# Input projection: other order of its pieces beside the hyena and the heads, and modulation's weights 1 MB at a time

## The chip, the cores and the metric

The kernel runs on one core of a Trainium2 chip. Its engines, TensorE (PE), VectorE (DVE), ScalarE (ACT), GpSimd (POOL) and SyncE (SP, which issues DMAs), each run their own queue in order and wait for one another by semaphores. The metric is the device time of one execution in microseconds (us).

## What is computed

One layer of a hybrid token mixer and an MLP, for 1024 latent and 256 context tokens of width 1024, in float32. One input projection feeds three groups: a Hyena long convolution, gated linear attention (GLA, 4 heads) and gated DeltaNet (GDN, 4 heads). GDN's q, k and v go through a convolution of 7 taps. Shifts, scales and gates (modulation) come from two vectors through `w_mod`.

```python
sh1, sc1, g1, sh2, sc2, g2 = jnp.split((silu_c @ w_mod[l] + b_mod[l])[:, None, :], N_MOD, axis=-1)
h = modulate(x, norm1_g[l], sh1, sc1)
...
zl_hy, zl_gla, zl_gdn = split_last(h @ w_in, IN_SIZES)
zc_hy, zc_gla, zc_gdn = split_last(hc @ w_in, IN_SIZES)
hy_lat = hyena_mix(zl_hy, rows, GRID_W, hy_conv_w, hy_conv_b, hyena_filters(h.shape[1], *hy_filter), hy_d)
gla_lat, gla_ctx = gla_branch(zl_gla, zc_gla, with_ctx_out, gla_w_a2, gla_b_a, gla_norm_g)
gdn_lat, gdn_ctx = gdn_branch(zl_gdn, zc_gdn, rows, with_ctx_out, gdn_conv_w, gdn_a_log, gdn_dt_bias, gdn_norm_g)
y_lat = jnp.concatenate([hy_lat, gla_lat, gdn_lat], axis=-1) @ w_out
...
x = x + g1 * y
x = x + g2 * sq_relu_mlp(modulate(x, norm2_g[l], sh2, sc2), w_mlp1[l], w_mlp2[l])
# inside gdn_prep: qkv = silu(short_conv(qkv, conv_w)); q, k l2-normed; inside the scan: solve (I - A) X = rhs, chunk by chunk
```

## The kernel before, in words

**Pieces.** The input projection is cut into 28 pieces of 128 output columns: hy0 to hy5 (hyena), gk, gv, gq, gg (GLA's k, v, q, gate), dk, dv, dq, dg (GDN's). `proj` makes a piece: `load_w` (L302) loads 512 KB of weights into `ws`, splits them into a rounded `wh` (ACT) and a rest `wl` (POOL), and PE sums three products (`mm3`) over 8 tiles of k into psum tiles `psb`, of which there are three. The latent tokens are two chunks of 512 columns, 24 matmuls each; pieces k and v have the context's 256 columns as a third chunk of 24. Pieces without convolution (`gla_piece`, `gate_piece`) are copied from psb by ACT. Pieces dq, dk and dv (`gdn_conv`, `taps`) start with an Identity by ACT, then DVE adds six taps for each chunk (`acc<-psb,vecs,acc`), ACT does a Silu, and `to_tokens` transposes the result on PE into the single psum tile `psd`, from where ACT copies it. A psb tile is free only when its last tap is done. `acc` has two buffers.

**Stages.** After the norm and the six hyena pieces come, in `run`:
1. the hyena (`long_conv` twice: DFT matmuls into `pss`, their operands made by ACT as `wrh` and DVE or POOL as `wrl`, sums `y` on DVE), with the first string of `SEQ` beside it, and after each piece two steps of modulation (`MODN`). A step of `mod_group` takes one tile of k: it loads weights into `mw` (SP's queue) and multiplies them on PE, four matmuls into one psum tile `psd` (of pool psm); after eight steps the sum is transposed into `modT`.
2. the four heads of GDN (`gdn_prep`), with the second string of `SEQ` (a digit is a head). `gdn_rows` first loads GDN's gates (`NT<-dz_gk`, SP's queue) and makes decays. A head loads k and q tokens, ACT makes 20 exps of 128x128 for either direction (`NT<-NT,cols`, `dm<-dm,cols`), and five rounds follow: k and q are transposed into `psp`, copied as `KQ` by ACT, multiplied into `psp`, and DVE makes `NT<-psp,dm` and `dm<-psp,dm` of it.
3. the inverse of all heads' triangular blocks (copies `i<-NT` on DVE and ACT, then many small matmuls into `psi`), with the third string as filler: a digit is one of the four decays of GLA (`gla_decays`, `acc<-acc` and a scan at L756), dg and gg are gates.
4. GLA, GDN's loops, the output projection and the MLP.

**What sets the order.** The code gives each instruction a priority by where it is written; taps and what follows them are moved ahead by `URGENT`. A scheduler then lays out each engine's queue by priorities and by when operands and buffers are expected to be ready. So a new order in `SEQ` moves instructions on all engines. Pools are closed at the end of a stage; tiles of a pool take turns (`mw`: two buffers of 128x1024).

Of the kernel before, what the change touches and what calls it, by code (L numbers as in the profile page):

```python
# [7 lines left out]
F32 = mybir.dt.float32  # L8
# [179 lines left out]
ENGC = {'eqf': 'vp', 'eqr': 'vp', 'qh0': 'vp', 'qh1': 'vp', 'ekf': 'vp', 'ekr': 'vp', 'kk': 'vp', 'qd0': 'avp', 'qd1': 'avp', 'A': 'va', 'te': 'vp', 'ke': 'vp', 'kt': 'va', 'A2': 'pva', 'q2': 'vp', 'og': 'va', 'ov': 'vp', 'mid': 'pva', 'pk': 'vp', 'pq': 'vp', 'tri': 'vp', 'KQ': 'va', 'C': 'avp', 'off': 'vp', 'Y': 'pva', 'T32': 'pva', 'Ya': 'vp', 'V': 'va', 'V64': 'va', 'pu': 'va', 'NT': 'avp', 'Yh': 'avp', 'V128': 'va', 'sp1': 'vp', 'sp0': 'vp', 'spc': 'vp', 'sps': 'vp', 'wl': 'vp', 'yg': 'vp', 'Sl': 'vp', 'ft': 'vp', 'oq': 'vp', 'qs': 'av', 'S2': 'avp', 'pl': 'vp', 'xr': 'vp', 'kd': 'vp', 'u': 'av'}  # L188
SEQ = ('gk1 gv0 dk0 dq0 gk0 dk1 dv2 gv1 dq1 dk2 gq0 dq2', '0 1 2 dv0 gq1 3 dv1 gv2', 'dg1 0 gg1 gg0 dg0 3 1 gg2 2 dg2')
MODN = 2  # L190
# [21 lines left out]
class Build:  # L212
# [99 lines left out]
    def run(self):  # L312
        tc, nc = self.tc, self.nc
        self._cst, self.y, self.nT, self.nS, self.rooms = {}, [], 0, 0, {i: i - 9 for i in range(4)}
        with ExitStack() as es:
# [38 lines left out]
            close(p0)  # L354
            h, mw = tp("hy", 1, True), tp("mw", 2, True)
            self.H = h[1]
# [82 lines left out]
    def mod_group(self, g, psum, pname, wpool, wnames):  # L439

        nc = self.nc
        ps = psum.tile([128, 512], F32, name=pname)
        for kt in range(8):
            for hf in range(2):
                w = wpool.tile([128, 1024], F32, name=wnames[hf])
                nc.sync.dma_start(w, self.I["wmod"][g, kt, hf])
                for q2 in range(2):
                    q = 2 * hf + q2
                    self.mm(ps[32 * q:32 * q + 32, :], self.cs32[:, kt, :], w[:, 512 * q2:512 * q2 + 512], kt == 0, kt == 7)
            yield  # L450
        ms = wpool.tile([128, 1024], F32, name=wnames[0])[:, :512]
        nc.scalar.copy(ms, ps)
# [10 lines left out]
    def mod_rest(self, psum, pool):  # L463

        for g in (1, 2):
            yield from self.mod_group(g, psum, "psd", pool, ("mw", "mw"))
        self.stt(self.A2, self.modT[:, 32:40, 0], 1.0, self.vec("n2"), ADD, MUL)
        for g in (20, 44):
            self.ts(self.modT[:, g:g + 4, 0], self.modT[:, g:g + 4, 0], -1.0, MUL)
        self.show("modT", self.modT)  # L470
        yield
# [1336 lines left out]
```

## Time and profile before

| | us |
|---|---|
| three runs | 1642.22, 1645.13, 1649.15 |
| median | 1645.13 |
| the profiled execution | 1637.75 |
| its span in the trace | 1636.0 |
| PE, DVE, ACT, POOL busy in the span | 1507.8, 1211.8, 803.2, 642.4 |

The profile is of one execution, so durations are set against its own time. "busy" of PE is the time in which a matmul is in the array; PEclk is the granted clock as a share of full speed (0.953 over the execution). A wait is put down to the instruction whose semaphore came last. In the trace, the hyena and the pieces beside it run from some 195 us to 366 us, the rest of the pieces and the heads to 577, the inverse to 690, and all that follows to the end.

### The profile page before, as it was taken

Reading aid. Unit: us, or ns where it says so; the run is one execution under the profiler, and the core shown is the slowest. Engines: PE = TensorE matmul, PEld = TensorE weight load, DVE = VectorE, ACT = ScalarE, POOL = GpSimd, SP = SyncE. Lnnn points to the kernel's source line nnn. Section 1 sums busy time; section 2 is a strip of 40 time slices with the busy share of each in tenths; the row PEclk is TensorE's granted clock in tenths of the full one; section 3 lists DMA queues with packets and bytes.
Section 4 is the critical chain, followed back from the end, with each engine's and each line's share of the span. In section 5 each row is a group of like instructions: output and inputs, shape, how many; then the busy total and the mean of one; then the engine's idle time right before and its main releaser. Section 6 shows DMA issues by size and latency. Waiting matters only on the chain. (4 is left out here: it accounts for less than half of the span.)

```text
span 1636.0 us, 26277 instructions
## 1 busy us (share of the span) xinstructions
PE 1507.8 (92%) x10160; PEld 1216.2 (74%) x10160; DVE 1211.8 (74%) x1827; ACT 803.2 (49%) x1462; POOL 642.4 (39%) x478
## 2 busy tenths in 40 slices
PE   7799999989999898768879799999999999999996
PEld 2378877767688676657779587788888888888886
DVE  5963589897575487676678878987679758974995
ACT  5432222315655644454556356554565456446554
POOL 0311141331434330131243254655556555655554
PEclk9999999999999997778889899999999999999998
DMA  8432777756566531267657934364455535453532
GB/s 296 135 110 91 259 256 263 238 180 210 165 205 197 165 134 46 75 192 209 182 148 226 309 103 104 103 155 129 104 132 124 149 87 153 103 136 96 135 72 103
DMA packets 116852, 256.81 MB, mean 157 GB/s; under 512 B 29431, under 2 KB 74919, under 8 KB 103800
## 3 DMA queue, kind: packets, MB, share of 16 engines
q1 hardware_dynamic: 88360, 175.42, 32.4%
q0 software_dynamic: 9808, 59.77, 16.4%
q10 hardware_dynamic: 18560, 19.94, 4.0%
q8 instruction: 80, 1.31, 0.3%
q14 instruction: 44, 0.36, 0.1%
HBM read 196.57 MB, written 41.75 MB: 146 GB/s over the span
## 5 line engine op out<-in xcount | busy, mean ns | idle before, releaser
L224 PE MATMUL psb<-T,S 128*128 128x512 f32 (+1 forms) x3072 | 693.3, 387 | 9.7 <-ACT T L292 6.0
L224 PEld LDWEIGHTS psb<-T,S 128*128 128x128 f32 x3072 | 571.0, 188 | 130.9 <-ACT T L292 6.8
L252 POOL TENSOR_TENSOR S<-wr,S 128x512 fp32r<-128x512 f32 x252 | 365.4, 1465 | 303.2 <-ACT S L292 302.6
L292 ACT CAST S<-wr 128x512 fp32r<-128x512 f32 x252 | 155.1, 620 | 150.0 <-PE psb L224 104.6
L224 PE MATMUL psb<-ahi,wh 128*128 128x512 f32 x448 | 184.5, 413 | 9.3 <-DVE acc L260 4.8
L224 PE MATMUL psb<-alo,wh 128*128 128x512 f32 x448 | 182.8, 408 | 0.0
L224 PE MATMUL psb<-ahi,wl 128*128 128x512 f32 x448 | 181.6, 405 | 0.0
L252 POOL TENSOR_TENSOR wl<-ws,wh 128x1024 fp32r<-128x1024 f32 x28 | 71.1, 2538 | 209.7 <-ACT wh L292 139.1
L260 DVE SCALAR_TENSOR_TENSOR acc<-psb,vecs,acc 128x504 f32<-128x504 f32 (+5 forms) x168 | 111.3, 678 | 49.8 <-ACT acc L264 47.5
L260 DVE SCALAR_TENSOR_TENSOR x<-psb,modT,x 128x512 f32<-128x512 f32 (+1 forms) x148 | 105.2, 727 | 40.2 <-PE psb L224 39.9
L252 DVE TENSOR_TENSOR T<-h,T 128x512 fp32r<-128x512 f32 x88 | 85.8, 1004 | 48.8 <-ACT T L292 47.3
L224 PEld LDWEIGHTS psb<-ahi,wh 128*128 128x128 f32 x448 | 87.8, 196 | 40.7 <-issue 9.1
L252 DVE TENSOR_TENSOR T<-ar,T 128x512 fp32r<-128x512 f32 x112 | 111.0, 1018 | 6.1 <-ACT T L292 5.9
L224 PEld LDWEIGHTS psb<-alo,wh 128*128 128x128 f32 x448 | 87.7, 196 | 26.1 <-issue 8.2
L224 PEld LDWEIGHTS psb<-ahi,wl 128*128 128x128 f32 x448 | 87.6, 196 | 22.5 <-issue 5.1
L292 ACT CAST T<-ar 128x512 fp32r<-128x512 f32 x112 | 68.5, 620 | 44.7 <-DVE ar L260 27.8
L252 POOL TENSOR_TENSOR lv<-cum 128x512 f32<-128x512 f32 x21 | 31.3, 1510 | 83.2 <-PE pss L224 36.9
L264 ACT ACTIVATE acc<-psb,vecs 128x512 f32<-128x512 f32 (+1 forms) x48 | 31.1, 663 | 64.1 <-PE psb L224 31.4
L292 ACT CAST T<-h 128x512 fp32r<-128x512 f32 x88 | 52.6, 619 | 19.5 <-DMA h<-dy 10.4
L264 ACT ACT_TABLE_LOAD x27 | 34.6, 1283 | 35.4 <-DVE acc L260 16.3
L1779 ACT COPY ar<-psb 128x512 f32<-128x512 f32 x48 | 28.2, 587 | 48.2 <-PE psb L224 47.6
L292 ACT CAST wh<-ws 128x1024 fp32r<-128x1024 f32 x28 | 29.3, 1045 | 44.8 <-PE psb L224 35.5
(332 smaller groups left out, 2597.7 us busy)
## 6 DMA issues: line engine op xcount, KB each, us to landing
wr<-in_w SPq DMA_DIRECT2D x40, 1024.0 KB, 4.8
wr<-in_w POOLq DMA_DIRECT2D x24, 1024.0 KB, 8.0
mw<-in_wmod SPq DMA_DIRECT2D x32, 512.0 KB, 5.1
ws<-in_win SPq DMA_DIRECT2D x28, 512.0 KB, 4.1
dft<-in_fw POOLq DMA_DIRECT2D x8, 1024.0 KB, 6.0
dft<-in_iv POOLq DMA_DIRECT2D x8, 1024.0 KB, 6.6
bd<-lv SPq DMA_DIRECT2D x32, 256.0 KB, 4.0
wr<-wr POOLq DMA_DIRECT2D x8, 1024.0 KB, 7.2
```

The costliest lines, as they stand in the source:

```text
L224: return self.nc.tensor.matmul(out, lhsT=lhsT, rhs=rhs, start=start, stop=stop, skip_group_check=more)
L252: return (eng or self.nc.vector).tensor_tensor(out, a, b, op)
L260: return (eng or self.nc.vector).scalar_tensor_tensor(out, a, s, b, op0=op0, op1=op1)
L264: return self.nc.scalar.activation(out, a, f, bias=bias, scale=scale)
L292: self.nc.scalar.copy(hi, src)
L1779: nc.scalar.copy(b[at[i]], ps)
```

## The change

Two edits. `SEQ` is reordered: the first string now has gk, gv and gq pieces in front and among the convolutions (gv2 and gq1 come into it, dv2 leaves it), and dv0, dv1, dv2 stand among the heads. And modulation's weights of the groups 1 and 2 come as one tile of 128x2048 (1 MB) for each step of k, in one buffer, in place of two tiles of 128x1024 (512 KB) in two buffers; the same four matmuls read it.

```diff
-SEQ = ('gk1 gv0 dk0 dq0 gk0 dk1 dv2 gv1 dq1 dk2 gq0 dq2', '0 1 2 dv0 gq1 3 dv1 gv2', 'dg1 0 gg1 gg0 dg0 3 1 gg2 2 dg2')
+SEQ = ('gk1 gv0 gk0 gv1 gq0 dk0 gv2 dq0 gq1 dk1 dq1 dk2 dq2', '0 1 2 dv0 dv1 3 dv2', 'dg1 0 gg1 gg0 dg0 3 1 gg2 2 dg2')
...
-            h, mw = tp("hy", 1, True), tp("mw", 2, True)
+            h, mw = tp("hy", 1, True), tp("mw", 1, True)
...
         for kt in range(8):
+            if len(wnames) == 1:
+
+                w = wpool.tile([128, 2048], F32, name=wnames[0])
+                nc.sync.dma_start(w.rearrange("p (h c) -> p h c", h=2), self.I["wmod"][g, kt].rearrange("h p c -> p h c"))
+                for q in range(4):
+                    self.mm(ps[32 * q:32 * q + 32, :], self.cs32[:, kt, :], w[:, 512 * q:512 * q + 512], kt == 0, kt == 7)
+                yield
+                continue
             for hf in range(2):
...
-        ms = wpool.tile([128, 1024], F32, name=wnames[0])[:, :512]
+        ms = wpool.tile([128, 2048 // len(wnames)], F32, name=wnames[0])[:, :512]
...
-            yield from self.mod_group(g, psum, "psd", pool, ("mw", "mw"))
+            yield from self.mod_group(g, psum, "psd", pool, ("mw",))
```

How the order of instructions moves is shown at three places.

**SP's queue where the hyena ends.** `mw<-in_wmod` are modulation's loads, `ws<-in_win` a piece's weights, `dy<-y` the hyena's results, `NT<-dz_gk` the gates that `gdn_rows` reads, `dtok_k<-acc` a finished convolution. Before:

```order
L446 DMA mw<-in_wmod 128x1024 x4
L305 DMA ws<-in_win 128x1024
L446 DMA mw<-in_wmod 128x1024 x2
L1365 DMA dy_109<-y_1381 128x1024
L1365 DMA dy_110<-y_1382 128x1024
L926 DMA NT_3544<-dz_gk_83 8x1280 x2
L446 DMA mw<-in_wmod 128x1024 x2
L305 DMA ws<-in_win 128x1024
L680 DMA dtok_k<-acc 1280x1x128
```

Now:

```order
L447 DMA mw<-in_wmod 128x2x1024 x2
L305 DMA ws<-in_win 128x1024
L1373 DMA dy_109<-y_1381 128x1024
L1373 DMA dy_110<-y_1382 128x1024
L447 DMA mw<-in_wmod 128x2x1024
L934 DMA NT_3553<-dz_gk_83 8x1280 x2
L447 DMA mw<-in_wmod 128x2x1024
L305 DMA ws<-in_win 128x1024
L688 DMA dtok_k<-acc 1280x1x128
```

Each load is now of 1 MB, and one of them, which needs the buffer of the load before, stands between the hyena's stores and the load of the gates.

**PE at head 0's rounds and at the last round of all heads.** `psp<-KQ` is the product of a round, `psp<-ident,k` and `psp<-ident,q` are its transposes, `psd<-ident,acc` the transposes of a convolution, and `psb<-ahi,wh` and the like the matmuls of a piece. Head 0's first round, before:

```order
L224 MATMUL psb<-ahi_970,wh 128x512
L224 MATMUL psb<-alo_971,wh 128x512
L224 MATMUL psb<-ahi_970,wl 128x512
L224 MATMUL psp<-KQ 128x256 x2
L287 MATMUL psp<-ident,k 96x128
L287 MATMUL psp<-ident,q 96x128
```

Now, the second and the third round:

```order
L224 MATMUL psp<-KQ 128x256 x2
L287 MATMUL psp<-ident,k 96x128
L287 MATMUL psp<-ident,q 96x128
L287 MATMUL psp<-ident,k 96x128
L287 MATMUL psp<-ident,q 96x128
L224 MATMUL psp<-KQ 128x256 x2
```

In before, pieces (gq0, dq2, dv0) stand between head 0's rounds; now its five rounds follow each other with only transposes between. At the last round of the last head, before:

```order
L224 MATMUL psb<-ahi_965,wl 128x512
L224 MATMUL psb<-ahi_970,wh 128x512
L224 MATMUL psb<-alo_971,wh 128x512
L224 MATMUL psb<-ahi_970,wl 128x512
L224 MATMUL psp<-KQ 128x128 x2
L224 MATMUL psb<-ahi_935,wh 128x512
```

Now:

```order
L224 MATMUL psd<-ident,acc 128x128 x2
L224 MATMUL psp<-KQ 128x256 x2
L287 MATMUL psp<-ident,k 96x128 x2
L224 MATMUL psp<-KQ 128x128 x2
L224 MATMUL psb<-ahi_935,wh 128x512
```

The matmuls ahead of the last round were those of gate piece gg1, and behind it came gg0; now gg1 comes behind it, and 17 matmuls of gg0 follow before the inverse's first.

**DVE at the start of the inverse.** `acc<-acc` and `acc<-smask,acc` are the subtraction and the scan of one decay of GLA, `i<-NT` the copies with which the inverse starts, `i<-i,vecs` its first operations. Before:

```order
L252 TENSOR_TENSOR acc<-acc 128x1280
L756 SCALAR_TENSOR_TENSOR acc<-smask,acc 128x1280
L260 SCALAR_TENSOR_TENSOR NT_3545<-psp,dm 128x256
L252 TENSOR_TENSOR dm<-psp,dm 128x256
L260 SCALAR_TENSOR_TENSOR NT_3546<-psp,dm 128x256
L252 TENSOR_TENSOR dm<-psp,dm 128x256
L260 SCALAR_TENSOR_TENSOR NT_3545<-psp,NT_3545 128x256
L260 SCALAR_TENSOR_TENSOR NT_3546<-psp,NT_3546 128x256
L237 COPY i_4562<-NT_3539 32x320 x2
```

Now:

```order
L237 COPY i_4568<-NT_3555 32x320 x2
L252 TENSOR_TENSOR acc<-acc 128x1280
L256 TENSOR_SCALAR i_4550<-i_4530,vecs 128x320 x2
L764 SCALAR_TENSOR_TENSOR acc<-smask,acc 128x1280
L256 TENSOR_SCALAR i_4588<-i_4568,vecs 128x320
L260 SCALAR_TENSOR_TENSOR i_4550<-i_4530,vecs,i_4550 128x320 x2
```

The decay's two operations stood ahead of the last rounds of the heads; now they stand behind the copies, between the inverse's own operations.

## Rows read from the trace of the kernel before

**Rows 1.** Windows by stage: window, length, busy us of each engine, PEclk, DMA, GB/s
```profile
195.00:366.00 171.00, 161.77 (x932) 125.89 (x931) 146.06 (x235) 45.52 (x75) 51.90 (x38) 0.97 0.71 246
366.00:425.00 59.00, 58.08 (x310) 40.94 (x308) 42.41 (x64) 30.77 (x47) 21.29 (x15) 1.00 0.67 215
425.00:577.00 152.00, 142.56 (x719) 118.27 (x720) 86.95 (x170) 96.51 (x189) 53.95 (x29) 0.98 0.59 177
577.00:690.00 113.00, 95.60 (x1561) 76.05 (x1559) 85.05 (x164) 53.93 (x84) 21.61 (x21) 0.79 0.17 67
```

**Rows 2.** PE's waits from 195 to 577: us in total, times, longest
```profile
PE psb L224 <- DVE acc L260: 4.8, 3, 2.7
PE pss L224 <- DVE wrl L252: 3.4, 2, 2.3
PE psp L224 <- ACT KQ L237: 3.1, 1, 3.1
PE pss L224 <- DVE y L260: 2.8, 1, 2.8
PE pss L224 <- ACT wrh L292: 2.3, 2, 2.1
PE psp L287 <- DVE dm L252: 1.3, 1, 1.3
PE psd L224 <- DMA mw<-in_wmod: 0.7, 2, 0.6
```

**Rows 3.** Windows of 4 us behind two of PE's longer waits, columns as above
```profile
336.00:340.00 4.00, 4.00 (x15) 3.21 (x14) 4.00 (x9) 0.69 (x1) 1.62 (x2) 0.57 1.05 414
...
445.00:449.00 4.00, 4.00 (x12) 3.15 (x11) 3.42 (x9) 3.08 (x9) 1.22 (x1) 0.57 0.44 107
```

**Rows 4.** PE's timeline at the inverse's start: row three starts 54 matmuls after row two
```profile
575.59 0.61 PE L224 MATMUL psp<-KQ 96*128 96x128 f32 x4
...
576.27 0.39 PE L224 MATMUL psb<-alo,wh 128*128 128x512 f32 x1
...
588.55 0.39 PE L224 MATMUL psb<-alo,wh 128*128 128x512 f32 x1
589.67 0.54 PE L224 MATMUL psi<-i,sel 128*128 128x300 f32 x2 [0.74 <-ACT i L292]
```

**Rows 5.** DVE's groups from 195 to 577: busy us, mean ns, idle before
```profile
L260 DVE SCALAR_TENSOR_TENSOR acc<-psb,vecs,acc 128x504 f32<-128x504 f32 x36 | 26.4, 739 | 0.7
...
L260 DVE SCALAR_TENSOR_TENSOR acc<-psb,vecs,acc 128x488 f32<-128x488 f32 x36 | 25.7, 720 | 27.6 <-ACT acc L264 27.3
...
L252 DVE TENSOR_TENSOR dm<-psp,dm 128x256 f32<-128x256 f32 x32 | 13.4, 421 | 0.7
L260 DVE SCALAR_TENSOR_TENSOR NT<-psp,dm 128x256 f32<-128x256 f32 x32 | 13.3, 417 | 26.9 <-PE psp L224 15.5 <-ACT ecol L264 6.3 <-ACT dm L264 4.9
```

**Rows 6.** ACT's timeline as head 0's exps begin: start, us
```profile
429.90 1.06 ACT L264 ACTIVATE acc<-acc 128x1024 f32<-128x1024 f32 x1
430.98 1.28 ACT L264 ACT_TABLE_LOAD   x1
...
433.42 2.15 ACT L264 ACTIVATE dm<-dm,cols 128x128 f32<-128x128 f32 x7
```

**Rows 7.** DVE's timeline before and at the inverse's start: start, us
```profile
567.56 1.49 DVE L252 TENSOR_TENSOR acc<-acc 128x1280 f32<-128x1280 f32 x1 [4.47 <-ACT acc L265]
569.09 2.82 DVE L756 TENSOR_TENSOR_SCAN acc<-smask,acc 128x1280 f32<-128x1280 f32 x1
...
577.02 9.01 DVE L237 COPY i<-NT 32x320 f32<-32x320 f32 x16
```

**Rows 8.** Tile mw's matmuls and landings, then tile wr's landings (1 MB each)
```profile
L224 PE MATMUL psd<-mw,cs x128: 592/617/1063, 210.1 to 422.0; 128*32 128x512 f32 x128
DMA to landing us min/median/max: 3.5/5.1/13.0
DMA to landing us min/median/max: 4.6/7.7/15.3
```

## The prediction

> **What bounds the kernel now.** The windows by stage come first [rows 1]. From 195 to 577 us TensorE is busy for 362.4 of 382 us: the projection's pieces, the hyena and the heads' KQ rounds share it, and what these stages cost is PE's work plus the waits in it. 577 to 690 is the inverse: PE is busy for 95.6 of 113 us there, with projection pieces as filler, so 17.4 us of PE are free; the chain of the inverse through DVE, ACT and PE sets the end. What comes later the change doesn't touch.
>
> Then PE's own waits [rows 2]. They make 19.6 us (9.2 us up to 366 us, the hyena's last matmul, and 0.92 + 9.44 = 10.4 us behind it). They are of two kinds: pss waits (y, wrl, wrh) are the hyena's, where DVE and ACT were late; psb waits are a projection piece without a free bank, because a convolution still held it. Third, behind a longer wait comes a stretch at half clock: granted 0.57 over 4 us at 336 and at 445 us [rows 3], so about 4 × 0.43 = 1.7 us more. There are five such stretches from 195 to 577 us, all at 0.57: two follow the hyena waits that I speak of below, two lie behind 366 us.
>
> Prices. A full-clock matmul of 512 columns takes (588.55 − 576.27)/54 = 0.227 us [rows 4], so a piece of 48 takes 10.9 us of PE and a piece with context (24 more of half the width) about 13.8 us. On DVE a convolution tap takes 0.72 to 0.74 us [rows 5], so a chunk of six costs 4.4 us; a piece has 12, with context 18.
>
> **The change part by part.** The total of matmuls, copies and taps stays as it is. What moves is listed by stage.
>
> (1) *Beside the hyena.* Of the convolutions' taps DVE gets only 14 of dk0's there until the hyena's last y, by the order, where before had 48 (dk0, dq0, dk1), so 34 taps, some 24 us, leave a stage in which DVE was busy for 146.1 of 171 us [rows 1]. The hyena's waits for y, wrh and the second for wrl [rows 2] were 2.8 + 2.1 + 1.1 = 6.0 us, and two half-clock stretches followed them, 3.4 us. All of it could go (−9.4), or nothing, if it is the hyena's own chain that is late. The second wait stood in the midst of dk1's taps, which speaks for the gain; the first began after slow operations of the hyena itself, which speaks against all of it. I take −7.7 us, halfway between 6.0 and 9.4.
>
> (2) *Behind the hyena.* The rest of dk0 and the convolutions dq0, dk1, dq1, dk2, dq2 and dv0 to dv2 now come between the hyena and the heads or within the heads, where ACT has the exps of the heads. I followed the order of the changed kernel by hand:
> - gq1's banks are freed by ACT copies that stand behind 20 exps of 0.31 us, a table load of 1.28 and a convolution's Silu of 1.06 [rows 6]: 8.5 us. PE has the next chunk to do meanwhile, 24 matmuls, 5.45 us. Left are 3.1 us, with the copy itself 3.7.
> - dq1 needs a bank that dk1's taps hold: as the longest such wait of before, 2.7 us [rows 2].
> - head 0's k transposes need psp behind dk2: as before's wait for KQ, 3.1 us [rows 2].
> - head 0's five rounds stand one behind the other on PE, with no piece between. A round takes two NT and two dm operations of DVE, 1.68 us [rows 5], so five take 8.4 us, and dk2's last chunk of taps, 4.4 us, comes ahead. PE has some 28 small matmuls of 0.15 us [rows 4] in it, 4.2 us. It waits 8.4 + 4.4 − 4.2 = 8.6 us.
> - the dm wait of 1.3 us and the smallest psb wait (4.8 − 2.7 − 0.8 = 1.3) stay [rows 2]: 2.6.
>
> That is 20.7 us of waits, where before has 10.4: +10.3. One more half-clock stretch than the two of before, +1.7. Together +12.0 us. From both sides: nothing, if DVE and ACT work off the pieces while PE runs ahead with gv2, dq0 and gq1 (168 matmuls come first), and +25, if every head's rounds wait as head 0's do.
>
> (3) *gg1.* Its 48 matmuls stood ahead of the last KQ round; now they stand behind it, beside the copies with which the inverse starts and in its free 17.4 us of PE. −10.9 us, as long as DVE and ACT set the inverse's pace; with PE as its bound, 0.
>
> (4) *The decay of GLA.* One subtraction and one scan, 1.49 + 2.82 us, ran on DVE at 567.6 us in a gap [rows 7], before the last rounds; now they stand behind the inverse's copies (9.0 us [rows 7]), among its first additions. DVE is in order, so the inverse's first matmul comes later by up to +4.3 us. ACT's half of the copies doesn't hide it. I take +4.3; 0 if the planner's order meets a DVE that would wait there anyhow.
>
> (5) *Filler in the later inverse.* gg2 and dg2 stand in runs of 23, 25 and 48 matmuls where runs of 16 and 32 stood. A chain matmul behind a run of 48 comes up to 16 × 0.227 = 3.6 us later. I take half, +1.8 (0 to 3.6).
>
> (6) *Modulation's weights.* 16 loads of 1 MB into one buffer take the place of 32 of 512 KB into two. A load now waits on SP's queue for the four matmuls of the tile before, and behind it stand the next weights, the y stores and head 0's NT load. The 128 modulation matmuls run from 210.1 to 422.0 us [rows 8]: 16 tiles, 13.2 us apart in the mean, the closest some 8 us by the matmuls that the order puts between them. Loads of 512 KB landed in 3.5/5.1/13.0 us (shortest, median, longest), the later loads of 1 MB, in a stage with less traffic, in 4.6/7.7/15.3 [rows 8]. The median is there in time, the longest is not. PE waited for these weights twice, 0.7 us together [rows 2]; I take +0.6 for the part left with 16 loads. The ends are −0.7 and +30 (eight of the sixteen late by half of 15.3 − 7.7, 3.8 us each).
>
> A rule of the Trainium skill speaks for this edit: the page "DMA: Bandwidth & Descriptors", section "Measured (HBM→SBUF, 128 partitions, SWDGE, issued from GpSimd)", wants transfers of 1 MiB and more and gives 6.15 us for 1 MB. By that figure no tile would be late, and this term would be 0 instead of +0.6. The landings of before agree for the median only; their longest are double the figure, because the rule speaks of a transfer alone and says nothing of one buffer.
>
> Sum: −7.7 + 12.0 − 10.9 + 4.3 + 1.8 + 0.6 = **+0.1 us**. The profiled run took 1637.75 us (its span is 1636.0), so 1637.9 us; that run is 7.4 us below the median of the three, 1645.13, so on the median's scale **1645 us**: no difference. A measurement of this kernel can tell about 0.5%, 8.2 us, from no change.
>
> **The rivals.**
> - *A: the late convolutions cost nothing.* PE's waits behind 366 us stay at before's 10.4 us, because DVE is only 57% busy from 425 to 577 [rows 1]. Then (2) falls to between 0 and 2: −7.7 − 10.9 + 4.3 + 1.8 + 0.6 + 1 = −11, and with the scan hidden, too, and all of (1), −17 and more. 1624 to 1636 us, at the most likely 1632. Against it: ACT is in order, and 20 exps stand ahead of the copies.
> - *B: the single buffer.* From the point at which a load of 1 MB takes longer than the 8 to 13 us between two tiles, each tile waits for its own landing, and PE, in order, with it. The stage has DMA at 0.71 of its time and 246 GB/s [rows 1], far more than where the 7.7 us were read. +10 to +30: 1655 to 1675 us.
> - *C: the pile on DVE and ACT.* dv0, dv1 and dv2 come within heads 1 to 3. If a chunk of taps, 4.4 us, stands in the way of each head's rounds, that adds 3 × 4.4 = 13 us to (2): 1653 to 1662 us. It decides when the taps, which are put ahead by priority, come to DVE before the NT and dm of a round that PE waits for. Against it: before had dv0 and dv1 within the heads as well, and its waits there are short.
>
> **How the numbers follow.** My forecast, no difference (1637 to 1653), has 0.42; A 0.31, B 0.12, C 0.15. A alone ends faster by more than 0.5%, B and C slower. The range of 8 in 10 leaves out the ends of A and B: 1626 to 1662 us.
>
> **What would show it.** (1): the pss waits before the hyena's last y, 9.2 us with the rest up to 366, fall to 3 or less. (2): PE's idle time from the hyena's last matmul to the last KQ round is about 21 us, with a cluster at head 0's rounds; 10 means A, over 30 means C. (3) and (4): from the inverse's first copy to its first psi matmul 12.7 us in before (577.0 to 589.7 [rows 4, 7]), 17 if the scan is in its way, and the inverse is no longer for gg1's sake. (6): waits for mw in PE's list stay below 1 us; many of 2 to 4 us mean B. The prediction is wrong if the order by hand isn't that of the clock: if ACT gets to gq1's copies before the exps are ready, (2) is half as large.

## The result: 1.4% slower

The changed kernel takes 1668.16 us (median of 4 runs, 1662.99 to 1673.37) where the one before, in the same comparison, takes 1643.68 (4 runs): a ratio of 1.0143, interval 1.0107 to 1.018. The forecast was 1645 and no difference, in a range of 1626 to 1662.

The windows of the changed kernel, cut at the hyena's last DFT matmul, head 0's first KQ round, the last KQ round, the first psi matmul of the inverse and the inverse's last one. (The first row, and the second and third together, can be held against [rows 1]: 195 to 366 and 366 to 577 us; head 0's first round comes at 440 us there.) Columns as in [rows 1]:

```profile
195.00:352.00 157.00, 146.07 (x901) 121.05 (x903) 124.77 (x198) 40.61 (x70) 52.63 (x37) 0.98 0.71 253
352.00:460.00 108.00, 95.25 (x494) 72.98 (x488) 59.97 (x92) 53.52 (x103) 33.71 (x24) 0.92 0.52 172
460.00:583.00 123.00, 107.08 (x518) 86.16 (x518) 87.26 (x169) 67.98 (x126) 43.25 (x22) 0.89 0.59 177
583.00:607.00 24.00, 17.70 (x68) 14.51 (x69) 17.69 (x34) 18.06 (x28) 11.90 (x9) 0.76 0.42 153
...
665.00:748.50 83.50, 55.92 (x1704) 47.11 (x1706) 49.23 (x84) 40.15 (x71) 11.12 (x10) 0.73 0.28 95
...
927.00:1671.00 744.00, 708.05 (x3154) 583.89 (x3154) 581.80 (x714) 392.23 (x695) 396.65 (x291) 0.97 0.48 126
```

And of the kernel before, the inverse from its first psi matmul to its last, and the last stage:

```profile
589.70:718.10 128.40, 98.94 (x1926) 80.88 (x1930) 91.68 (x169) 59.66 (x92) 18.46 (x16) 0.76 0.23 79
...
900.90:1636.00 735.10, 704.72 (x3155) 580.99 (x3154) 577.30 (x715) 392.38 (x695) 395.04 (x291) 0.98 0.48 127
```

To be seen there: behind the hyena (second and third row) PE is idle for 12.8 + 15.9 = 28.7 us where [rows 1] gave 10.4, and the granted clock is 0.92 and 0.89 where it was 1.00 and 0.98. Between the last KQ round and the inverse's first matmul stand 24 us, in before 13.5 (576.2 to 589.7). The inverse itself runs for 141.9 us from its first psi matmul to the last, in before 128.4. The last matmul of GDN comes at 926.7 us against 900.9, 25.8 us later, and that is near the medians' difference, 24.5 us. The last row, where nothing is changed, is 9 us longer than in before, although PE, DVE, ACT and POOL do the same operations in the same order there; the profiled execution (span 1671.6) is the slowest of its four, and that of before (1637.75 us) is faster than its four. So two executions can differ by some 10 us in a stage that is the same, and such a difference between two traces says little by itself.

The 25.8 us, stage by stage (change of each stage's length in these two traces): up to the last KQ round +6.4, from there to the first psi matmul +10.5, the inverse +13.5, behind it −4.6. The first of these hides most: PE had done 47 matmuls of pieces fewer by then (gg1, 10.7 us), so that stage in truth lost some 17 us, and some 11 more that modulation's edit gave back (see e2 below).

PE's waits from the hyena's end to the inverse's start, to be held against [rows 2]:

```profile
PE psp L224 <- ACT KQ L237: 8.3, 8, 2.9
PE psb L224 <- ACT acc L264: 8.0, 2, 6.7
PE psb L224 <- DVE acc L260: 7.1, 4, 4.7
PE psp L287 <- DVE dm L252: 3.8, 2, 2.8
PE psd L287 <- ACT acc L729: 3.1, 2, 2.0
PE psp L287 <- DVE NT L252: 2.2, 1, 2.2
PE psp L287 <- DVE NT L949: 1.4, 1, 1.4
```

There is no single wait: taps hold psb banks (7.1), rounds of the heads wait for KQ and dm (12.1), GDN's decays (NT) come late. The 6.7 us of the second row lie ahead of the inverse's first psi matmul. ACT's timeline shows what happened:

```profile
580.93 0.37 ACT L237 COPY KQ<-psp 96x256 f32<-96x256 f32 x1 [0.92 <-PE psp L287]
588.56 1.63 ACT L264 ACTIVATE acc<-psb,vecs 128x512 f32<-128x512 f32 x3 [7.26 <-DMA dtok_v<-acc]
590.21 1.28 ACT L264 ACT_TABLE_LOAD   x1
591.51 1.27 ACT L264 ACTIVATE acc<-acc 128x1280 f32<-128x1280 f32 x1
592.79 1.28 ACT L265 ACT_TABLE_LOAD   x1
...
594.09 1.36 ACT L265 ACTIVATE acc<-acc,cst 128x1280 f32<-128x1280 f32 x1
595.36 7.51 ACT L237 COPY i<-NT 32x320 f32<-32x320 f32 x16
```

GLA's first decay needs an `acc` buffer that dv2, now the last convolution, still holds: its store `dtok_v<-acc` has to land first. ACT waits 7.3 us for that, then does the decay for 6.8 us, two table loads among it, and only then its half of the inverse's copies, which begin at 595.4 although the last KQ round is over at 582.6.

### The profile page after: what moved, and what is told of

Same layout as the page of the kernel before. It is cut to its first block, busy times and chain, and to the rows that moved or that the text cites. A ratio compares the mean times of both kernels' runs of the same rounds, so it can differ in the third digit from the quotient of the medians.

```text
span 1671.6 us, 26230 instructions
## 1 busy us (share of the span) xinstructions
PE 1514.6 (91%) x10160; PEld 1229.7 (74%) x10160; DVE 1214.4 (73%) x1827; ACT 801.5 (48%) x1461; POOL 648.6 (39%) x478
## 5 line engine op out<-in xcount | busy, mean ns | idle before, releaser
L252 DVE TENSOR_TENSOR T<-h,T 128x512 fp32r<-128x512 f32 x88 | 90.5, 1057 | 45.8 <-ACT T L292 44.8
L292 ACT CAST wh<-ws 128x1024 fp32r<-128x1024 f32 x28 | 29.4, 1049 | 66.8 <-PE psb L224 54.6
L252 POOL TENSOR_TENSOR lv<-cum 128x512 f32<-128x512 f32 x21 | 27.8, 1344 | 85.5 <-PE pss L224 30.5
L1787 ACT COPY ar<-psb 128x512 f32<-128x512 f32 x48 | 28.2, 588 | 50.2 <-PE psb L224 49.7
L264 ACT ACT_TABLE_LOAD x26 | 33.4, 1283 | 29.0 <-DVE acc L260 14.5
```

The lines of the kernel that those rows point to most:

```text
L252: return (eng or self.nc.vector).tensor_tensor(out, a, b, op)
L264: return self.nc.scalar.activation(out, a, f, bias=bias, scale=scale)
L292: self.nc.scalar.copy(hi, src)
L1787: nc.scalar.copy(b[at[i]], ps)
```

## The experiments

The theories, as the expectations number them. Theory 1: the inverse's start (a decay ahead of ACT's copies) and gg1 as filler inside the inverse. Theory 2 (rival B of the prediction): the single 1 MB buffer. Theory 3 (rival C's kind): late convolutions pile up on DVE and ACT, and PE waits behind the hyena. Theory 4 and theory 7: it is dv2 behind all heads, or the set of pieces beside the hyena, whatever their order. M and L: what the 1 MB tile itself does.

The table gathers all runs. "Beside" and "behind" are PE's waits, in us, from 195 us to the hyena's last DFT matmul and from there to the last KQ round (sums of waits over 0.1 us in each trace); "to psi" is from the last KQ round to the first psi matmul, "inverse" from that to the last one; "filler" counts the matmuls of pieces behind the last KQ round; "groups" is the number of uninterrupted groups in which modulation's 128 matmul records come. All but the ratio are read from one execution each.

| kernel | ratio (interval) | beside | behind | last KQ at | to psi | inverse | filler | groups |
|---|---|---|---|---|---|---|---|---|
| before | 1 | 9.2 | 10.3 | 576 | 13.5 | 128.4 | 191 | 30 |
| changed | 1.0143 (1.0107 to 1.018) | 10.9 | 28.2 | 583 | 24.0 | 141.9 | 240 | 19 |
| e1 order alone | 1.0231 (1.0181 to 1.0281) | 8.7 | 22.4 | 591 | 20.3 | 140.5 | 239 | 30 |
| e2 modulation alone | 0.998 (0.995 to 1.0009) | 8.9 | 14.5 | 574 | 13.9 | 124.3 | 152 | 16 |
| e3 decay later | 1.0131 (1.0094 to 1.0169) | 9.1 | 26.4 | 588 | 11.8 | 131.9 | 178 | 19 |
| e4 dv2 back | 1.0135 (1.0103 to 1.0166) | 9.0 | 26.0 | 589 | 17.5 | 132.7 | 217 | 19 |
| e5 halves first | 0.9984 (0.996 to 1.0008) | 9.3 | 10.1 | 575 | 13.2 | 127.6 | 191 | 30 |
| e6 dk, dq early | 0.9967 (0.9936 to 0.9997) | 9.1 | 12.8 | 581 | 11.7 | 123.6 | 123 | 16 |
| e7 changed, no taps | 1.0223 (1.0156 to 1.0289) | 11.4 | 11.1 | 603 | 31.6 | 126.1 | 96 | 19 |
| e8 e2, no taps | 1.0113 (1.0044 to 1.0182) | 9.3 | 13.2 | 598 | 25.6 | 104.3 | 96 | 18 |
| e9 alternating | 1.0128 (1.0073 to 1.0183) | 15.4 | 26.4 | 594 | 12.6 | 130.3 | 197 | 16 |
| e10 convolutions last | 1.0187 (1.0136 to 1.0237) | 9.5 | 33.6 | 585 | 20.7 | 138.9 | 240 | 18 |
| e11 convolutions first | 1.0102 (1.0052 to 1.0151) | 9.5 | 25.6 | 595 | 12.6 | 128.8 | 197 | 21 |
| e12 gates by the heads | 1.0128 (1.0076 to 1.018) | 8.5 | 21.1 | 591 | 25.4 | 127.4 | 144 | 19 |
| e13 changed, 4 banks | 1.0124 (1.0067 to 1.018) | 13.1 | 29.4 | 608 | 13.7 | 121.3 | 145 | 21 |
| e14 e2, 4 banks | 1.0336 (1.0302 to 1.037) | 13.9 | 25.8 | 641 | 22.4 | 123.4 | 52 | 24 |
| e15 one step | 1.0108 (1.0075 to 1.0141) | 17.1 | 13.6 | 591 | 14.6 | 123.3 | 171 | 20 |
| e16 gq1 in the inverse | 0.9916 (0.9882 to 0.9949) | 8.6 | 13.9 | 573 | 13.0 | 123.4 | 172 | 16 |
| e17 e16, 512 KB | 1.0056 (1.0015 to 1.0096) | 9.7 | 11.9 | 589 | 13.3 | 121.3 | 157 | 31 |
| e18 e16, gq0 too | 1.0104 (1.0055 to 1.0153) | 8.3 | 24.3 | 559 | 12.6 | 137.3 | 293 | 16 |

### Each edit alone (e1, e2)

e1 is the kernel before with the new `SEQ`, e2 the changed kernel with the old one:

```diff
 # e1: before.py
-SEQ = ('gk1 gv0 dk0 dq0 gk0 dk1 dv2 gv1 dq1 dk2 gq0 dq2', '0 1 2 dv0 gq1 3 dv1 gv2', ...)
+SEQ = ('gk1 gv0 gk0 gv1 gq0 dk0 gv2 dq0 gq1 dk1 dq1 dk2 dq2', '0 1 2 dv0 dv1 3 dv2', ...)
```

> Only the order of the pieces is changed; modulation's weights come as in the kernel before (512 KB, two buffers). Theory 1 (the inverse's start: a decay's ACT work, which waits for dv2's store, stands ahead of ACT's copies, and gg1 comes inside the inverse): ratio to before 1.011 to 1.015, the distance from the last KQ round to the first psi matmul about 24 us as in the changed kernel (13.8 in before). Theory 2 (the single 1 MB buffer of modulation): ratio 1.000 to 1.004. Theory 3 (late convolutions hold PE behind the hyena): ratio 1.011 to 1.015 too.

> Only modulation's weights are changed (1 MB, one buffer); the order of the pieces is that of before. Theory 2: ratio 1.010 to 1.015, with waits of PE for mw of some 2 us each at many tiles. Theories 1 and 3: 0.998 to 1.003, at most 2 or 3 us of waits for mw, as in the changed kernel (2.7 against 0.7).

The order alone is slower than both edits together (1.0231, some 38 us against 24; no theory had put it above 1.015), and modulation's edit alone isn't slower (0.998, an interval that holds 1). Rival B, the single buffer, is out: PE waited 2.7 us for mw in the changed kernel, and its 1 MB loads landed in 4.8/6.2/14.2 us (shortest, median, longest), the median and the longest between the two rows of landings in [rows 8].

What no theory had was that modulation's edit **helps** beside the hyena: e2 reaches the hyena's last DFT matmul at 352 us, before at 366.5, with the same 282 piece matmuls done since 195 us and four modulation records fewer. PE's waits until then are as long (8.9 us against 9.2), so it is PE's own work that got shorter:

```profile
195.00:352.00 157.00, 148.02 (x923) 123.67 (x921) 141.76 (x229) 44.37 (x74) 54.60 (x37) 0.98 0.74 259
```

The timelines of PE show why, first of before (three groups of modulation's records), then of e2:

```profile
235.13 1.05 PE L224 MATMUL psd<-mw,cs 128*32 128x512 f32 x4
...
270.65 1.05 PE L224 MATMUL psd<-mw,cs 128*32 128x512 f32 x2
...
329.40 1.06 PE L224 MATMUL psd<-mw,cs 128*32 128x512 f32 x8
```

```profile
244.32 1.06 PE L224 MATMUL psd<-mw,cs 128*32 128x512 f32 x8
```

Eight records (the four matmuls of a k tile; a float32 matmul shows as two records) take 1.06 us when they follow one another, four take 1.05, and two, a single matmul, take 1.05 as well. Each of the four has 32 stationary columns (`128*32`) and writes another 32 partitions of the psum tile, and by these times they run beside one another if nothing stands between. With two tiles of 512 KB the scheduler mostly put two of the four, other work, and the other two: 30 groups of about 1 us. With one tile there are 16 groups in e2: some 14 us of PE less. The Trainium skill has this in "TensorEngine Tiling (Array Packing)", section "Theoretical Speedup": up to 4x for a dimension of 32 or less; the rows agree that four take no longer than two. The size of the load is not what does it: the group of eight at 329.40 us is one of before, with 512 KB loads, and the changed kernel, with 1 MB, has groups of four that take 1.05 us too:

```profile
261.54 1.05 PE L224 MATMUL psd<-mw,cs 128*32 128x512 f32 x4 [2.29 <-DMA mw<-in_wmod]
```

In e2 the 14 us end up as 3 by the ratio: the last KQ round comes 2 us earlier with 39 more piece matmuls done, then the inverse has less filler, and GDN's last matmul comes 6.2 us earlier than in before.

### The inverse's start (e3, e4)

e3 puts the first decay two gates later, e4 does dv2 beside the hyena again and gq1 and gv2 among the heads:

```diff
 # changed kernel, e3
-'dg1 0 gg1 gg0 dg0 3 1 gg2 2 dg2'
+'dg1 gg1 gg0 0 dg0 3 1 gg2 2 dg2'
 # changed kernel, e4
-('gk1 gv0 gk0 gv1 gq0 dk0 gv2 dq0 gq1 dk1 dq1 dk2 dq2', '0 1 2 dv0 dv1 3 dv2', ...)
+('gk1 gv0 gk0 gv1 gq0 dk0 dv2 dq0 dk1 dq1 dk2 dq2', '0 1 2 dv0 gq1 3 dv1 gv2', ...)
```

> The changed kernel, but in the third string the first decay stands two gates later (dg1 gg1 gg0 0 in place of dg1 0 gg1 gg0). Its ACT work then comes behind ACT's copies of the inverse, and gg1's matmuls come ahead of the last KQ round. Theory 1: the last KQ round to the first psi falls from 24 to about 14 us, and the time by 10 to 20 us: ratio to before 1.002 to 1.008. Theories 2 and 3: 1.012 to 1.015, since waits for mw and behind the hyena stay.

> The changed kernel, but dv2 is done beside the hyena again and gq1 and gv2 among the heads (first string gk1 gv0 gk0 gv1 gq0 dk0 dv2 dq0 dk1 dq1 dk2 dq2, second that of before). Theory 3: PE's waits behind the hyena fall from some 30 to 10 to 15 us, and the ratio to 1.002 to 1.007. Theory 1: the decay's ACT work still stands ahead of the copies and gg1 half inside the inverse, so 1.007 to 1.013; only the wait for dv2's store is gone. Theory 2: 1.012 to 1.015.

In e3 the copies start as soon as they can, as ACT's timeline shows, and the way from the last KQ round to the first psi matmul is 11.8 us in place of 24:

```profile
585.28 0.59 ACT L264 ACTIVATE acc<-psb 128x512 f32<-128x512 f32 x1
585.77 7.52 ACT L237 COPY i<-NT 32x320 f32<-32x320 f32 x16
```

So the decay is what held the copies up. Its worth in time is small: a ratio of 1.0131 against 1.0143, with intervals that overlap, and in the traces GDN's last matmul 9.6 us earlier (917.1 against 926.7). gg1 now stands ahead of the last round, which comes 5 us later; the waits behind the hyena are 26.4 us, in the changed kernel 28.2. e4 removes the wait for dv2's store (17.5 us to psi) and lands at the same ratio. Theory 1 explains about a third of the loss by the traces, and by the ratios it isn't told from nothing.

### Where the convolutions stand (e6, e9, e10, e11, e15)

All five keep the changed kernel's second and third string and the same pieces in the first, in another order:

```diff
 # changed:  'gk1 gv0 gk0 gv1 gq0 dk0 gv2 dq0 gq1 dk1 dq1 dk2 dq2'
+# e6   'gk1 gv0 dk0 dq0 gk0 dk1 gv2 gv1 dq1 dk2 gq0 gq1 dq2'
+# e9   'gk1 dk0 gv0 dq0 gk0 dk1 gv1 dq1 gq0 dk2 gv2 dq2 gq1'
+# e10  'gk1 gv0 gk0 gv1 gq0 gv2 gq1 dk0 dq0 dk1 dq1 dk2 dq2'
+# e11  'dk0 gk1 dq0 dk1 gv0 dq1 dk2 gk0 dq2 gv1 gv2 gq0 gq1'
+# e15  'gk1 gv0 gk0 gv1 dk0 dq0 dk1 gv2 dq1 dk2 gq0 gq1 dq2'
```

> The changed kernel with before's first string, in which only dv2 is given up for gv2 and gq1 (gk1 gv0 dk0 dq0 gk0 dk1 gv2 gv1 dq1 dk2 gq0 gq1 dq2): the convolutions dk and dq are early again, dv2 is late. By the order, no decay stands ahead of ACT's copies here, and gates come ahead of the last KQ round. Theory 3 (late dk and dq hold PE and the heads): waits and half-clock stretches behind the hyena as with modulation's edit alone, first KQ round at about 447 us, ratio 0.996 to 1.003. Theory 4 (dv2 behind all heads costs the time by itself): 1.008 to 1.014.

> The changed kernel, with the same pieces in the first string, but convolutions and others in turn (gk1 dk0 gv0 dq0 gk0 dk1 gv1 dq1 gq0 dk2 gv2 dq2 gq1). Theory 3 (the fewer of dk and dq are done when the hyena ends, the more of DVE's and ACT's work piles up before head 0, and PE waits for it): PE's waits from the hyena's last DFT matmul to the first psi matmul at most 18 us (35 in the changed kernel, 14 to 15 where dk and dq came early), ratio to before 0.996 to 1.004. Theory 7 (it is the set of pieces beside the hyena, or dv2 at the end): 1.010 to 1.015.

> The changed kernel with every convolution of the first string behind all others (gk1 gv0 gk0 gv1 gq0 gv2 gq1 dk0 dq0 dk1 dq1 dk2 dq2): the cause that theory 3 names, made larger. Theory 3: waits of 38 us and more between the hyena and the first psi, ratio 1.016 to 1.025. Theory 7: as the changed kernel, 1.012 to 1.016.

> The changed kernel with the convolutions of the first string ahead of the others, as far as the gates' source gk1 allows (dk0 gk1 dq0 dk1 gv0 dq1 dk2 gk0 dq2 gv1 gv2 gq0 gq1). Theory 3: the other end of the scale, waits of 15 us or fewer behind the hyena, though beside the hyena PE may wait longer for y, wrh and wrl than the 10 us of before; ratio 0.992 to 1.002. Theory 7: 1.010 to 1.015.

> The order with dk and dq early (ratio 0.9967) with one step towards the changed kernel's: gk0 and gv1 come ahead of dk0 and dq0 (gk1 gv0 gk0 gv1 dk0 dq0 dk1 gv2 dq1 dk2 gq0 gq1 dq2). If the loss grows with each convolution that is put off, 1.002 to 1.009, with waits of PE from the hyena to the last KQ round of 16 to 24 us; if there is a threshold, 0.994 to 1.001 or 1.010 and more.

e6 settles the main point: with dk and dq early, the same pieces beside the hyena and dv2 at the end cost nothing (0.9967 against 1.0143; e2, with before's order and the same modulation edit, has 0.998). Theories 4 and 7 are out. What e6 doesn't part is the waits from the rest: with this order the scheduler also puts gates ahead of the last KQ round and no decay ahead of ACT's copies (123 filler matmuls, 11.7 us to psi). Its waits behind the hyena:

```profile
PE psp L224 <- ACT KQ L237: 3.9, 4, 1.3
PE psp L287 <- DVE NT L964: 2.7, 2, 1.6
...
PE psb L224 <- DVE acc L260: 0.8, 1, 0.8
```

At the other end, e10 (all convolutions last) is the slowest of the five, and of all waits the two that theory 3 names are largest there:

```profile
PE psb L224 <- DVE acc L260: 12.1, 2, 10.7
PE psp L224 <- ACT KQ L237: 10.6, 5, 3.4
```

So psb behind DVE's taps goes 0.8, 7.1, 12.1 us from e6 to the changed kernel to e10, and the ratio 0.997, 1.014, 1.019. That this one wait sets the ratio isn't so: e4, with late convolutions too, has none of it behind the hyena and waits as long for KQ, psd and the decays (26 us, 1.0135). And theory 3 as a scale, the earlier the convolutions the better, falls with e9, e11 and e15: they put dk0 and dq0 as early as e6 or nearly so, and are 1.0 to 1.3% slower than before. Each has longer waits at a place of its own. e9, two rows beside the hyena and behind it:

```profile
PE pss L224 <- DVE wrl L252: 11.8, 4, 4.6
```

```profile
PE psp L287 <- DVE NT L964: 10.1, 2, 6.5
```

PE waits there for the hyena's wrl and for GDN's decays. That the taps cause it isn't shown: in the 8 us before the longest wait for wrl ends DVE does the hyena's own operations, a small one of modulation's and no tap, and of the longest wait for NT (6.5 us, to 419.9) two taps of 0.7 us are all that is theirs. In e15 it is one wait of 10 us beside the hyena, in which modulation's next matmul stood in PE's queue until DVE had read its psum tile, behind operations of the hyena and taps:

```profile
PE psd L224 <- DVE modT L252: 10.0, 1, 10.0
```

What is common to the slow orders of this section is, by their lists of waits, the kind of loss and not the place: an instruction stands at the head of PE's queue and waits for an operation of DVE or ACT that comes late. What makes it late was not followed through in each.

### The taps taken away (e7, e8)

```diff
-        acc = self.conv(n, 7, "gdncw", i, ctx)
+        acc = self.conv(n, 1, "gdncw", 7 * i + 3, ctx)
```

e7 is the changed kernel and e8 is e2, and both leave out six of the seven taps of every convolution of GDN (two executions of each).

> The changed kernel without the six outer taps of GDN's convolutions (DVE has none of acc<-psb,vecs,acc there), so its output is not the layer's. Theory 3, in the form that DVE's taps hold the psb banks: the loss against the same with before's order (next kernel) shrinks from some 27 us to less than 10. If it is the heads' exps on ACT or the order by itself, 15 us and more remain.

> The kernel with modulation's edit alone (before's order), and as in the run beside it without the six outer taps of GDN's convolutions. It is the baseline for that run. Theory 3 by DVE's taps: the two are within 10 us; by ACT or order: this one is 15 us faster or more.

The total difference stays (18 us), so by the letter of the expectation DVE's taps are not it. By stage it is otherwise. From the hyena's end to the last KQ round, e7 first, then e8:

```profile
350.00:603.00 253.00, 241.87 (x1181) 188.22 (x1180) 75.78 (x136) 156.56 (x262) 86.65 (x48) 0.94 0.55 176
```

```profile
350.00:598.00 248.00, 234.72 (x1172) 184.73 (x1170) 70.32 (x135) 138.79 (x248) 87.19 (x48) 0.96 0.57 180
```

PE is idle for 11.1 and 13.3 us: without taps the changed order has no more waits there than the old one. In the kernels with taps it was 28.2 against 14.5. So the additional waits behind the hyena go with the taps, though the scheduler laid out the rest anew as well. The two kernels still differ, by 5 us up to the last KQ round (granted clock 0.94 against 0.96) and most of all behind it, where the scheduler filled the inverse in another way in either (31.6 against 25.6 us to psi, 126.1 against 104.3 us of inverse). Why both are slower than the kernels with taps stays open: their gates come early, and only 96 filler matmuls are left.

### Filler and the inverse (e12, e16, e17, e18)

e12 is the changed kernel with gg0 and gg1 among the heads. e16 is before's first string with dv2 and gv2 exchanged and gq1 moved into the third, with modulation's edit; e17 is e16 without that edit; e18 moves gq0 as well.

```diff
+# e12  second string '0 gg0 1 gg1 2 dv0 dv1 3 dv2', third 'dg1 0 dg0 3 1 gg2 2 dg2'
+# e16  ('gk1 gv0 dk0 dq0 gk0 dk1 gv2 gv1 dq1 dk2 gq0 dq2', '0 1 2 dv0 dv1 3 dv2', 'dg1 0 gq1 gg1 gg0 dg0 3 1 gg2 2 dg2')
+# e18  as e16, without gq0 in the first string, third 'dg1 0 gq0 gq1 gg1 gg0 dg0 3 1 gg2 2 dg2'
```

> The changed kernel with the gate pieces gg0 and gg1 among the heads (second string 0 gg0 1 gg1 2 dv0 dv1 3 dv2), not in the inverse. Head 0's rounds still follow each other by the order. If the gates inside the inverse carry the loss (theory 1, second half): first psi to the inverse's last matmul falls from 142 to about 122 us and the ratio to 1.000 to 1.005. Theory 3: the waits between the hyena and the last KQ round stay near 28 us, and the ratio at 1.008 to 1.015.

> Before's order with dv2 and gv2 exchanged, modulation's edit, and gq1 moved into the inverse's filler (first string gk1 gv0 dk0 dq0 gk0 dk1 gv2 gv1 dq1 dk2 gq0 dq2; third dg1 0 gq1 gg1 gg0 dg0 3 1 gg2 2 dg2). If PE has room in the inverse, the last KQ round comes some 10 us earlier, the inverse is hardly longer: 0.990 to 0.996. If filler there costs its full 10.9 us, as gg1 did in the changed kernel: 0.996 to 1.002, with the inverse 8 us longer or more.

> The kernel with gq1 in the inverse (ratio 0.9916) without modulation's edit: 512 KB loads in two buffers, as in before. If the 1 MB tile is worth its 14 us of PE time in part: ratio 0.995 to 1.000, modulation's matmuls at about 236 ns each again. If it is worth nothing by itself: 0.990 to 0.993.

> The kernel with gq1 in the inverse, and gq0 moved there as well, with modulation's edit. If PE still has room in the inverse: 0.984 to 0.991, and from the first psi matmul to the inverse's last at most 5 us more than the 123.5 us with gq1 alone. If it is full: the inverse grows by some 10 us and the ratio stays at 0.990 to 0.997.

e12: the inverse falls from 141.9 to 127.4 us, the last KQ round comes 8 us later and the ratio stays, so gates are moved rather than saved. e16 is **faster than both kernels**: 1628.99 us, 0.9916 (0.9882 to 0.9949). Its windows from the hyena's end to the last KQ round, and from the inverse's first psi matmul on:

```profile
354.00:451.50 97.50, 93.66 (x501) 73.52 (x501) 58.69 (x96) 51.44 (x82) 32.17 (x21) 0.98 0.58 188
451.50:573.00 121.50, 111.45 (x548) 90.67 (x547) 70.18 (x140) 81.35 (x162) 48.22 (x24) 0.93 0.61 192
...
586.00:648.50 62.50, 55.86 (x233) 41.71 (x235) 46.49 (x91) 29.14 (x32) 4.41 (x5) 0.78 0.14 53
648.50:709.50 61.00, 38.77 (x1626) 34.29 (x1625) 39.91 (x74) 27.00 (x56) 8.71 (x8) 0.67 0.28 97
```

PE idles for 13.9 us behind the hyena, the last KQ round is at 573 us with 172 filler matmuls left, and the inverse takes 123.4 us. Against e6, which has gq1 beside the hyena, the inverse ends 6.7 us earlier (709.3 us, e6 716.0). That this is what makes e16 faster isn't shown: GDN's last matmul comes at 895.9 us, in e6 at 896.7 and in e2 at 894.7. The difference lies behind it, in code that none of these edits touches, and what makes that stage shorter stays open. First e16, then e2:

```profile
895.90:1626.70 730.80, 704.96 (x3154) 581.48 (x3154) 573.96 (x714) 391.78 (x695) 399.03 (x291) 0.99 0.46 124
```

```profile
894.70:1637.50 742.80, 709.90 (x3155) 585.67 (x3154) 580.37 (x715) 391.91 (x695) 393.51 (x291) 0.98 0.47 126
```

e17 shows what the 1 MB tile is worth in a good order: without it 1.0056, 31 groups again, last KQ round at 589 in place of 573, GDN's last matmul 14.0 us later. e18 goes too far: behind the hyena PE waits for 24.3 us, 12.3 of them for KQ copies, which fits that fewer pieces are left to stand between the rounds, and 293 filler matmuls are left for an inverse of 137.3 us. It still ends its inverse at 709.2 us, as e16 does: moving 121 matmuls more (27.5 us of PE) gained nothing there and lost nothing. Its loss of some 30 us against e16 comes later. GDN's last matmul is 21 us behind e16's, and right behind the inverse PE is busy for 27.5 of 51 us where e16 has 41.1:

```profile
709.00:760.00 51.00, 27.48 (x472) 25.03 (x472) 38.14 (x59) 24.33 (x52) 12.56 (x9) 0.72 0.88 238
```

In the kernels with taps and three banks the inverse takes 121 to 133 us with up to 217 filler matmuls (e2, e6 and e16, with 123 to 172: 124 us), and 137 to 142 us with 239 and more (e18, with the most, 137).

### Three runs that didn't tell what they should (e5, e13, e14)

e5 (both 512 KB halves loaded first, then four matmuls) was meant to separate the adjacency of the matmuls from the size of the load:

```diff
+            ww = []
             for hf in range(2):
...
+                ww.append(w)
+            for q in range(4):
+                self.mm(..., ww[q // 2][:, 512 * (q % 2):512 * (q % 2) + 512], kt == 0, kt == 7)
```

> The kernel before (512 KB loads, two buffers, its order of pieces), but of each k tile both halves are loaded first, and the four matmuls follow one another. Theory M (what the 1 MB tile gives is that the four matmuls of a tile, each on its own 32 columns of the array, run beside one another): PE's time for a modulation matmul falls from 236 ns to about 120, as in the run with modulation's edit alone (157.3 us from 195 us to the hyena's last DFT matmul against 171.5), so about 157 here too, and a ratio of 0.995 to 1.001. Theory L (the gain is in the loads): 171 as in before.

The scheduler parted the matmuls again (30 groups), so the kernel is the one before in all but name, and its ratio says so. That adjacency is what counts rests on the rows above (groups of two, four and eight with 512 KB loads), not on e5.

e13 and e14 give the projection a fourth psb bank, taken from the hyena's pss:

```diff
-ps("psb", 3), ps("psd", 1), ps("pss", 3, True)
+ps("psb", 4), ps("psd", 1), ps("pss", 2, True)
```

> The changed kernel with four psb banks in place of three, taken from the hyena's pss (two in place of three). If the taps' hold on the banks is what PE waits for behind the hyena: its waits from there to the last KQ round fall from 28 to 15 us and less, psb behind DVE's acc from 7.1 to below 1.5, and the ratio to before to 0.995 to 1.005. If the waits come from the heads' own chains (exps, KQ copies, decays): they stay over 22 us and the ratio at 1.010 and more. In both, the hyena may get slower for want of its third bank, by up to some 10 us.

> Modulation's edit with before's order, and four psb and two pss banks, as the baseline of the run beside it. Bank theory: it gains little by the fourth bank (psb behind DVE's acc is only 1.1 us there), and the hyena's price shows alone: ratio 0.995 to 1.005, and the run beside it comes within 6 us of it. Theory of the heads' chains: the run beside it stays 15 us and more behind.

In e13 psb behind DVE's acc falls to 1.7 us, but the waits as a whole stay at 29.4: the hyena ends at 416 us, GDN's decays (`NT`) come late and take the place of the taps (10.2 us). The order that is good with three banks is 3.4% slower with four. So a bank taken from the hyena does not heal it. What the bank alone would do isn't shown, since the hyena pays for it: it ends at 425 us in e14, where e2 has 352.

## Why the prediction was wrong, step by step

- **(1) Beside the hyena, −7.7: wrong.** DVE did get less to do (124.8 of 157 us, 146.1 of 171 before), and the waits didn't fall: 10.9 us against 9.2. The wait for y went (2.8 to 0.4 us), wrh's rose from 2.3 to 4.8, and a wait for mw of 2.3 came. What PE waits for is the hyena's own chain (wrh, wrl: 8.2 of the 10.9 us), the case that the step named ("or nothing") and then gave no weight in its −7.7. The granted clock there is 0.98, 0.97 before, so of the two half-clock stretches little was gained.
- **(2) Behind the hyena, +12.0: right in kind, too small.** The waits rose by 17.9 us (10.3 to 28.2) where +10.3 was summed, and the time at half clock from 195 us to the last KQ round, worked out from the granted clock, rose from 17 to 50 us where one stretch of 3.4 us was added. Of the single terms, head 0's rounds have the size that was said (7.9 us in their eight waits from 460 to 477 us, 8.6 expected), in part by luck: 3.7 of them are waits for ACT's KQ copies, and the term had DVE alone. The psb waits behind taps are 7.1 us where 4.0 were summed, those behind ACT's copies 1.3 where 3.7 were, and a KQ wait of 4.1 us comes at 515 us, not at head 0. What failed is the list: the late decays of GDN (4.3 us), the transposes behind psd (3.1) and the clock were not in it. It was a by-hand walk through the order of one engine at a time.
- **(3) gg1 into the inverse, −10.9: wrong.** The last KQ round was to come earlier by that; it had 47 piece matmuls fewer ahead of it. But the inverse grew by 13.5 us: 240 filler matmuls where 191 stood. The 17.4 us in which PE is idle in [rows 1] were not room for it: in the changed kernel's inverse PE still has 27.6 us of idle time from 665 to 748 us. That filler is what lengthens it e12 shows: with the late start still there (25.4 us to psi) and 96 filler matmuls fewer, the inverse is back at 127.4 us. How, by filler that stands in PE's queue ahead of the chain's next matmul, is argued and not shown. From e16 to e18 121 more filler matmuls, 27.5 us of PE, made the inverse 13.9 us longer, about half their time.
- **(4) The decay, +4.3: right place, wrong engine and size.** DVE's scan is there, but what counts is ACT, of which the step has only the copies: the same decay's three operations, with two table loads, stand ahead of them, and wait for dv2's store. +10.5 us to the first psi matmul.
- **(5) Filler in the later inverse, +1.8:** a part of the 13.5 us of (3); no run shows it by itself.
- **(6) Modulation, +0.6: wrong in sign.** The loads behave nearly as expected (landing 6.2 us in the median, PE's waits 2.7 us where 1.3 were allowed). The 7.7 us of [rows 8], which the step calls an agreement with the 6.15 us that it quotes, are a quarter above it. What the step left out is PE: the edit puts a tile's four matmuls together, which saves some 11 us there (30 groups to 19), 14 in e2. e1 and e17 show it in the time: 0.9% between e1 and the changed kernel (1.0231 to 1.0143), some 14 us, and 1.4% between e17 and e16. The sentence "the total of matmuls stays as it is" was true of their number and not of their time.

So the forecast's zero was a sum of six terms of which two gains didn't come (−18.6), two losses were too small by half, and one gain was unseen. The rival that came nearest is C, by its place (PE behind late DVE and ACT work in the heads' stage) and its time, 1653 to 1662; that dv0 to dv2 in the heads would be its cause is not what the runs show: the place of dk and dq among the first string's pieces is (e6 against the changed kernel, with the same dv pieces in the same place). B, with a chance of 0.12, is refuted by e2.

What stays open: no run shows why just this order of dk and dq is good; e9, e11 and e15 say that the neighbours of a good order are not good. Nor is it shown how the 25.8 us divide between the waits behind the hyena, the clock, the late decay and the filler: a new order moves all four.

## What to carry to other kernels

In a kernel whose engines are all ordered by a scheduler, a move of pieces should be followed on every in-order queue at the points where the next stage starts, ACT above all: a small off-path operation ahead of the stage's first copies can hold the stage up for what it waits for (7.3 us here) besides what it takes. PE's idle time in a chain-bound stage isn't room for filler without a price; count the filler matmuls in it and see at which count the stage grows. Follow a gain to the end of the kernel: e18 is level with e16 at the inverse's end and 21 us behind at GDN's. And matmuls that use different strips of the array belong together: a larger load can be worth its while for the order that it forces on TensorE.

## What the runs showed of the hardware

Matmuls with 32 stationary columns each, put on four different strips, take 1.06 us for the four of a tile (8 records) when adjacent, two of them 1.05 us and one alone 1.05: parted in two, they cost double. The 1 MB loads into modulation's tile landed in 4.8/6.2/14.2 us in the changed kernel and 4.8/7.9/14.4 in e2, against 3.5/5.1/13.0 for 512 KB ones at the same place [rows 8]. And more waits went with more time at the lower clock level: from 195 us to the last KQ round TensorE was granted half its clock for 17 us where PE waited for 19.5 us in all (before), and for 50 us where it waited for 39.1 (changed).
